# Fewer, larger stores at the end, one load merged, and a tenth pair of tiles turned by VectorE, in a matmul with scale and add

## The chip, the cores and the metric

One core of one Trainium2 chip. The metric is device time in microseconds (us); most executions of one kernel agree within 0.3%. The span is the time from the first to the last of the program's own instructions in the profiled execution; it is about 1.8 us shorter than the device time. All comparisons are between runs of state "fast".

## The reference

```python
batch, m, k, n = 16, 512, 1024, 768
# x [batch, m, k], weight [k, n], add_value [batch, m, n], all float32; scale = 0.1
return (scale * np.matmul(x, weight) + add_value).astype(np.float32)
```

Rows are taken together: 8192 rows, 64 tiles of 128 rows. Read are 61.87 MB, written 25.17 MB.

## The kernel before

The order of all transfers is a list. "x", "w" and "a" load tiles of x, of the weight and of add_value; "o" stores whole tiles, "l" and "r" the left and right columns of one; the numbers are the first tile and how many. All are issued by SyncE, on one queue:

```python
STREAM = [
    ("x", 0, 3), ("w", 0, 2), ("w", 2, 2), ("w", 4, 2), ("x", 3, 1), ("w", 6, 2),
    ("a", 0, 3), ("x", 4, 4), ("a", 3, 1), ("x", 8, 4), ("a", 4, 4), ("x", 12, 4),
    # ... cut ...
    ("o", 40, 8), ("o", 48, 8), ("o", 56, 4), ("o", 60, 1), ("o", 61, 1), ("o", 62, 1),
    ("l", 63, 1), ("r", 63, 1),
]
PAIRS = [14, 19, 24, 29, 34, 39, 44, 49, 54]
```

A tile of x arrives as float32; GpSimd casts it to bfloat16. It then has to be turned for the matmul. For most tiles TensorE transposes it (four 128x128 transposes) and ScalarE copies the result from PSUM. The tiles that PAIRS names (each entry and the one after it) are turned by VectorE in 32x32 blocks, four calls of four instructions per pair, spread over four steps:

```python
def step():
    t = done["step"]
    if t < T - 1:
        for j in range(KJ):                     # KJ = 8
            if j == KJ // 2:
                if t + 1 not in in_pair:
                    transpose(t + 1)            # TensorE, then ScalarE
                cast_to(min(t + AHEAD, done["x"] - 1))     # GpSimd
                if t + 7 in PAIRS:
                    cast_pair(t + 7)            # GpSimd
            product(t, j, BOTH)                 # 128x512 and 128x256
        finish(t, BOTH[0], 0, N)                # VectorE: ao = mm * scale + ao
        for a in range(P // 32):
            if t + 6 - a in PAIRS:
                turn_pair(t + 6 - a, a)         # VectorE
    # ... last tile: columns 0:512 first, then 512:768 ...
```

add_value is loaded into the tile `ao`, overwritten with the result in place and stored from there.

## Time and profile before

| | before |
|---|---|
| device time, median of 3 | 210.95 us |
| span | 209.2 us |
| TensorE / VectorE busy | 196.4 / 131.1 us |
| bytes moved by DMA | 87.2 MB |

In a table by stage the columns are the stretch, its length, busy time (and number of instructions) of each engine, the granted TensorE clock, the DMA share and GB/s. In the list of DMA issues the last number is us from issue to landing.

### The profile page before, as it was taken

What the parts mean: (1) busy time and instruction counts of PE and PEld (TensorE: products, weight loads), DVE (VectorE), ACT (ScalarE), POOL (GpSimd) and SP (SyncE); (2) the same over time, 40 slices, a digit from 0 to 9 for tenths busy, and PEclk for the clock granted to TensorE, in tenths of its full rate; (3) what the DMA queues carried; (4) which work ended last, traced back from release to release, by engine and by line L of the source; (5) the groups of instructions that cost most, each with busy time, mean ns of one, the idle gap of its engine ahead of it and who ended that gap; (6) DMA issues with size and microseconds to landing.
All of it is one profiled execution on the core that took longest, in us unless ns stands there. A gap on an engine that the chain in (4) does not pass through costs nothing.

```text
span 209.2 us, 2988 instructions
## 1 busy us (share of the span) xinstructions
PE 196.4 (94%) x1218; PEld 119.5 (57%) x1218; DVE 131.1 (63%) x223; ACT 49.3 (24%) x52; POOL 63.2 (30%) x69
## 2 busy tenths in 40 slices
PE   7599499999999999999999999999999999999990
PEld 2355256656665666566665666565666656666550
DVE  0545413309969969898697886949994994223340
ACT  2513113233103112113032031121130230332310
POOL 1310536420292090503903606303503039100000
PEclk9889979999999999999999999999999999999997
DMA  6999999999999999999999999999999999999993
GB/s 233 418 431 447 423 408 441 451 445 407 404 481 410 418 432 418 432 451 415 437 417 436 436 421 425 442 434 423 423 432 445 445 409 418 432 447 426 409 402 152
DMA packets 5485, 87.21 MB, mean 417 GB/s; under 512 B 608, under 2 KB 736, under 8 KB 2016
## 3 DMA queue, kind: packets, MB, share of 16 engines
q1 hardware_dynamic: 5472, 87.03, 97.7%
q8 instruction: 9, 0.15, 0.3%
q14 instruction: 4, 0.03, 0.0%
HBM read 61.87 MB, written 25.17 MB: 416 GB/s over the span
## 4 chain that ended last, share of the span: by engine, by line
PE 90%; DMA 3%; DVE 2%; ACT 1%; POOL 0%; issue 0%; ACTq 0%; POOLq 0%
PE mm L168 80%; PE tp L146 10%; DMA xs<-in_x_dram 3%; DVE ao L235 1%; ACT xt L152 1%; DVE ao L204 1%; POOL xb L136 0%; DVE xb L132 0%; DVE ao L176 0%; ACTq L152 0%; POOLq L136 0%
## 5 line engine op out<-in xcount | busy, mean ns | idle before, releaser
L168 PE MATMUL mm<-w_bf,xt 128*128 128x512 bf16 (+1 forms) x736 | 130.8, 331 | 0.6 <-DVE ao L204 0.4
L168 PEld LDWEIGHTS <-xt 128*128 128x128 bf16 x736 | 69.6, 99 | 50.8 <-ACT xt L152 11.4
L176 DVE SCALAR_TENSOR_TENSOR ao<-mm,ao 128x768 f32<-128x768 f32 (+2 forms) x62 | 58.3, 944 | 54.1 <-PE mm L168 35.3
L152 ACT COPY xt<-tp 128x1024 bf16<-128x1024 bf16 (+1 forms) x49 | 46.6, 961 | 146.0 <-PE tp L146 146.0
L120 DVE STREAM_TRANSPOSE vt<-vx 32x256 f32<-32x256 f32 x144 | 62.7, 435 | 6.2 <-POOL vx L109 4.0
L136 POOL CAST xb<-xs 128x1024 bf16<-128x1024 f32 x43 | 43.2, 1040 | 56.2 <-DMA xs<-in_x_dram 46.5
L168 PE MATMUL mm<-w_bf,vt 128*128 128x512 bf16 (+1 forms) x288 | 49.7, 326 | 0.0
L168 PEld LDWEIGHTS <-vt 128*128 128x128 bf16 x288 | 28.2, 98 | 17.5
L109 POOL CAST vx<-xs 128x1024 bf16<-128x1024 f32 x18 | 18.3, 1040 | 53.8 <-DVE vt L120 44.7
L146 PE MATMUL tp<-identity,xb 128*128 128x128 f32 x184 | 28.3, 277 | 5.4 <-POOL xb L136 3.0
L146 PEld LDWEIGHTS tp<-identity,xb 128*128 128x128 f32 x184 | 21.7, 143 | 12.1 <-POOL xb L136 3.4
L104 DVE CAST w_bf<-ao 128x768 bf16<-128x768 f32 x8 | 4.1, 557 | 3.8 <-DMA ao<-in_weight_dram 3.8
L132 DVE CAST xb<-xs 128x512 bf16<-128x512 f32 x3 | 1.9, 696 | 5.6 <-DMA xs<-in_x_dram 5.6
L94 PE MATMUL warm<-zeros 128*128 128x512 bf16 x10 | 4.3, 617 | 1.2 <-DVE zeros L82 1.2
L134 POOL CAST xb<-xs 128x512 bf16<-128x512 f32 x2 | 1.6, 834 | 5.5 <-DMA xs<-in_x_dram 5.5
L94 PEld LDWEIGHTS <-zeros 128*128 128x128 bf16 x10 | 1.3, 140 | 3.4 <-issue 2.2
L204 DVE TENSOR_SCALAR ao<-mm 128x768 f32<-128x768 f32 x2 | 1.8, 952 | 2.3 <-PE mm L168 2.3
L235 DVE TENSOR_TENSOR ao<-ao 128x768 f32<-128x768 f32 x3 | 2.7, 950 | 0.0
L134 ACT CAST xb<-xs 128x512 bf16<-128x512 f32 x1 | 0.6, 618 | 4.8 <-DMA xs<-in_x_dram 4.8
L134 ACT ACT_TABLE_LOAD x1 | 1.3, 1283 | 0.7 <-PEq L279 0.7
L201 ACT ACTIVATE ao<-mm 128x768 f32<-128x768 f32 x1 | 0.8, 817 | 0.0
L82 DVE MEMSET zeros<- 128x256 uint32 x1 | 0.3, 272 | 0.9 <-PEq L279 0.9
(6 smaller groups left out, 0.9 us busy)
## 6 DMA issues: line engine op xcount, KB each, us to landing
xs<-in_x_dram SPq DMA_DIRECT2D x6, 4096.0 KB, 27.3
ao<-in_add_value_dram SPq DMA_DIRECT2D x7, 3072.0 KB, 24.3
out_dram<-ao SPq DMA_DIRECT2D x7, 3072.0 KB, 31.2
xs<-in_x_dram SPq DMA_DIRECT2D x3, 2048.0 KB, 22.0
ao<-in_weight_dram SPq DMA_DIRECT2D x4, 768.0 KB, 9.5
xs<-in_x_dram SPq DMA_DIRECT2D x1, 1536.0 KB, 6.0
ao<-in_add_value_dram SPq DMA_DIRECT2D x1, 1536.0 KB, 23.7
out_dram<-ao SPq DMA_DIRECT2D x1, 1536.0 KB, 11.7
```

Source lines behind the costliest of these rows:

```text
L94: nc.tensor.matmul(warm[:, 0:CUT], zeros[:, 0:P], zeros, start=True, stop=True)
L104: nc.vector.tensor_copy(w_bf[:, j + i, :], ao[:, s + i, :])
L109: nc.gpsimd.tensor_copy(vx[:, i, :], xs[:, (t0 + i) % X_SLOTS, :])
L120: nc.vector.transpose(vt[b:b + 32, :, 32 * a:32 * a + 32], pairs[32 * a:32 * a + 32, :, b:b + 32])
L134: other(xb[:, K // 2:K], src[:, K // 2:K])
L136: nc.gpsimd.tensor_copy(xb, src)
L146: nc.tensor.transpose(tp[:, c, :], pairs[:, c * P:(c + 1) * P], identity)
L152: nc.scalar.copy(dst[:, c:c + q, :, :], src[:, c:c + q, :, :])
L168: nc.tensor.matmul(mm_tiles[t, cols[0]][:, n0:n1], lhs(t, j), w_bf[:, j, n0:n1], start=(j == 0), stop=(j == KJ - 1))
L176: nc.vector.scalar_tensor_tensor(a, mm_tiles[t, part][:, n0:n1], float(scale), a, op0=mybir.AluOpType.mult, op1=mybir.AluOpType.add)
L204: nc.vector.tensor_scalar(ao[:, EARLY_AT + t, :], mm_tiles[t, BOTH[0]][:, 0:N], float(scale), None, op0=mybir.AluOpType.mult)
L235: nc.vector.tensor_add(ao[:, t, :], ao[:, EARLY_AT + t, :], ao[:, t, :])
```

## The change

Its intent: fewer transfers (38 become 34) with longer rows, and less work on TensorE near the end, so that it is done sooner.

```diff
-    ("a", 0, 3), ("x", 4, 4), ("a", 3, 1), ("x", 8, 4), ("a", 4, 4), ("x", 12, 4),
-    ("a", 8, 8), ...
+    ("a", 0, 3), ("x", 4, 4), ("a", 3, 5), ("x", 8, 4), ("x", 12, 4), ("a", 8, 8),
     # ... the middle of the list has the same order ...
-    ("o", 56, 4), ("o", 60, 1), ("o", 61, 1), ("o", 62, 1), ("l", 63, 1), ("r", 63, 1),
+    ("o", 56, 4), ("o", 60, 3), ("o", 63, 1),
-PAIRS = [14, 19, 24, 29, 34, 39, 44, 49, 54]
+PAIRS = [14, 19, 24, 29, 34, 39, 44, 49, 54, 59]
```

(The store of a part of the columns, "l" and "r", goes out of the code.)

## The prediction

> **What bounds the kernel now**
>
> I read the page first (sections 1 to 4), then the table by stage, then SyncE's own waits and its timeline at the end, then the DMA issues of the last 5 us, and last VectorE and GpSimd from 160 us on, where the new pair has to fit.
>
> The page:
>
> ```profile
> span 209.2 us, 2988 instructions
> PE 196.4 (94%) x1218; PEld 119.5 (57%) x1218; DVE 131.1 (63%) x223; ACT 49.3 (24%) x52; POOL 63.2 (30%) x69
> DMA  6999999999999999999999999999999999999993
> q1 hardware_dynamic: 5472, 87.03, 97.7%
> q8 instruction: 9, 0.15, 0.3%
> PE 90%; DMA 3%; DVE 2%; ACT 1%; POOL 0%; issue 0%; ACTq 0%; POOLq 0%
> ```
>
> Two resources look full: TensorE 94%, and the 16 DMA engines 97.7%. The chain of waits gives 90% to TensorE, but that chain ends at the last instruction of a compute engine and does not know what the stores do after it. The table by stage (its last two columns are the DMA share and GB/s) decides:
>
> ```profile
> 60.00:100.00 40.00, 40.00 (x259) 24.72 (x257) 34.23 (x62) 9.11 (x9) 14.68 (x16) 1.00 1.01 432
> 185.00:200.00 15.00, 15.00 (x99) 9.40 (x98) 4.79 (x5) 4.71 (x6) 0.00 (x0) 1.00 1.00 427
> 200.00:205.00 5.00, 3.57 (x22) 1.88 (x20) 2.07 (x3) 0.74 (x1) 0.00 (x0) 1.00 0.95 390
> 205.00:209.20 4.20, 0.00 (x0) 0.00 (x0) 0.00 (x0) 0.00 (x0) 0.00 (x0) 0.70 0.26 97
> ```
>
> DMA is at 1.00 in every stage from 7 us to 200 us. After 205 us no compute engine does anything, and DMA still drains. The end in three views (chain of waits, SyncE's timeline, DMA issues from 203.9 us on):
>
> ```profile
> 203.61 0.42 DVE ao L176
> ```
> ```profile
> 203.45 0.94 SPq L262 DMA_DIRECT2D out_dram<-ao  x2
> ```
> ```profile
> out_dram<-ao SPq DMA_DIRECT2D x1, 128.0 KB, 4.1
> ```
>
> VectorE finishes the last tile at 204.03. The last store (128 KB, issued at 204.06) lands 4.1 us later, at about 208.2, though 128 KB at 432 GB/s is 0.30 us. It waited in the queue behind earlier stores. So the end is set by when the DMA engines have moved 87.03 MB, and TensorE has roughly 3 us of slack there. The span closes about 1 us after the landing, and the measured time is 1.75 us above the span (210.95 against 209.2); I keep both constant.
>
> One more thing from the trace's records: each transfer's landing is 16 completions, one per DMA engine, and they spread. For the last store they run from 205.66 to 208.20, the second last at 207.38. Early on (before 28 us) the spread is 0.33 us. It grows by about 1 to 1.5 us on one engine each time an instruction-refill packet appears: nine of 16,384 bytes on q8, about 20 us apart from 28.0 to 189.9 us, which took 1.0 to 1.1 us each, and smaller ones on q14. After the one at 189.9 the latest engine falls another 1.3 us behind, so it was hit twice. That engine alone sets the last 0.8 us.
>
> **What the Trainium skill says**
>
> - "DMA: Bandwidth & Descriptors", Where 436 GB/s comes from: the SBUF side of the 16 engines tops out at 435 GB/s. The 432 GB/s above agrees; there is nothing left to gain in rate.
> - The same page, Anatomy of one DMA: about 2.0 us fixed plus bytes over 436e9 (it states this for the GpSimd path). Here, from SyncE, the first load (1536 KB) took 6.0 us to land: 3.6 for the bytes and 2.4 fixed. Close. With a queue in front of it the fixed part is hidden, as successive landings show.
> - The same page, Why a DMA increments its semaphore by 16 and not by 1: the engines finish independently. The spread of 2.5 us at the end agrees.
> - "Runtime: NRT & Kernel Launch", Instruction fetch mechanics: refills come in 16 KiB blocks of 256 instructions, "mostly hidden". The nine blocks agree in size and come every 250 to 270 TensorE records; hidden they are not here, since each takes time of a DMA engine that has none spare.
>
> **The change part by part**
>
> 1. *Stores of the tail.* Removed: three of 384 KB, one of 256 and one of 128. Added: one of 1152 KB, one of 384 KB. Same bytes. Each engine handles 8 rows of each transfer. From the packet records (medians): 3072 B 121 ns, 2048 B 84, 1024 B 46, 9216 B 352, and 9 ns for a completion. Per engine before: 8 x (3 x 121 + 84 + 46) = 3944 ns; after: 8 x (352 + 121) = 3784 ns; minus three completions, 27 ns. Saved 0.19 us. Cross-check from landings: the five land over 208.20 - 204.47 = 3.73 us; one 1536 KB store just before took 3.64. So 0.09 is the least, 0.19 the most. It lies on the path.
>
> 2. *add_value 3 to 7 in one.* Before 3072 B + 12288 B rows: 121 + 460 = 581 ns; after one of 15360 B, interpolated between 460 (12288 B) and 912 (24576 B): 573. Eight rows: 0.06 us, plus a completion, 0.07. On the path, since DMA never idles from then on. It moves order: x 8 to 11 now waits behind 1536 KB more of add_value, so it lands at about 34.2 instead of 30.6; add_value 3 lands at about 27.9 instead of 24.2, and 4 to 7 at 27.9 instead of 34.2. Tile 8's TensorE transposes begin at 38.50; GpSimd would cast it by 35.3: 3.2 us to spare. Tile 3's last step on VectorE slips from 26.77 to about 28, and its accumulator is wanted only by tile 6 at about 33. Nothing on the path; tiles 4 and 5 even leave VectorE earlier, as their 6.6 us wait for add_value goes away.
>
> 3. *Tenth pair, tiles 59 and 60.* The order of instructions shows eight transposes (and two ACT copies) fewer on TensorE, sixteen 32x256 transposes more on VectorE, two GpSimd casts into vx in place of two into xb. TensorE: a tile takes 2.63 + 0.44 us with transposes and 7.83 / 3 = 2.61 without (chain), so 2 x 0.46 = 0.9 us earlier at its end. That is not on the path: it moves the issue of the last stores from 201.96 and 204.06 to about 201.1 and 203.15. VectorE: 16 x 435 ns = 7.0 us, in a stretch where it waits on TensorE:
>
> ```profile
> 179.49 0.96 DVE L176 SCALAR_TENSOR_TENSOR ao<-mm,ao 128x768 f32<-128x768 f32 x1 [2.08 <-PE mm L168]
> 170.60 6.95 POOL L136 CAST xb<-xs 128x1024 bf16<-128x1024 f32 x7 [11.69 <-DMA xs<-in_x_dram]
> ```
>
> Its input is late, since x 56 to 63 lands at 170.5. GpSimd casts 56, 57, 58, then 59 and 60, done at 175.6. The first four transposes follow tile 53, whose last step ends at 174.8: VectorE waits 0.8 us, then 1.78 us, so tile 54's step starts at 177.4 instead of 176.45. Tile 55's is late by 0.6, 56's by 0.3, 57's by none; the last transposes end at 185.6. TensorE needs tile 59 at about 188.6, and three accumulators cover the 1 us. Nothing on the path.
>
> Sum: 0.09 to 0.19 plus 0.07, about 0.2 us of 210.95. **Predicted 210.7 us.**
>
> **The rivals**
>
> - *TensorE sets the end.* For it: 94% and the chain. Then 0.9 us from the pair less the loss of the split last store: about 210.0. Against it: 4.1 us to land 128 KB, and 4 us of DMA after the last instruction.
> - *The merged store starves the DMA engines.* The 1152 KB store cannot start before tile 62 is done, at about 201.1, plus some 2.4 us until data moves: 203.5. Engines that are ahead (the first finishes the 1536 KB store at 201.0) idle, which does not matter; the latest finishes it at 204.47 and sees its next work already queued. Margin 1 us, and it exists partly because of the pair. If the fixed part were 1 us longer: 211 to 211.5.
> - *Refills land elsewhere.* The change takes 16 TensorE instructions away and gives VectorE 16. If the refill at 189.9 hit another engine, or dropped out, the end would come at the second-last engine: 0.8 us earlier, 209.9. If one more hit the latest engine: 1.1 to 1.3 us later, about 212. I count on the same nine: about 180 TensorE records follow the last of them, and the 16 removed stand near it. That is the largest uncertainty.
> - *Late VectorE work stalls TensorE.* It would have to cost over 3 us before the DMA end moves. Unlikely.
>
> **Range and chances**
>
> Most mass is within 0.3 us of 210.7; the refill rival stretches downward to 209.9, starving and refills upward to 211.3. Eight in ten: 210.1 to 211.2. A 2% gain is 206.7 us, below what 87 MB at 432 GB/s plus start and end allow (201.5 + 2.4 + 1 + 1.75 = 206.6): under 1%. A 2% loss is 215.2: it needs a stall of over 4 us in the DMA stream, 1%.
>
> **What the profile after would show**
>
> Right: span about 209.0, DMA busy 9 in every slice but the ends, VectorE's last step about 203.1, the last store issued near 203.15 and landing near 208.0 (some 4.8 us); the 1152 KB store issued at about 201.1; TensorE busy about 0.9 to 2 us lower; VectorE about 138; no wait of TensorE longer than now. Wrong: a DMA share visibly under 1.00 before 200 us; a landing of the last store that moves with VectorE's end; another count or place of q8 packets, or an end that moves by 0.8 us or more.

## The result, and the profile after

210.88 us (median of 6, 210.45 to 211.07) against 210.93 (6 runs of the kernel before beside it, 210.59 to 211.10). Ratio 0.9996, 95% interval 0.9984 to 1.0009: the same. A ratio here is the mean time of one kernel's fast runs over that of the other's of the same rounds, so not quite the ratio of the medians.

The page of the changed kernel, the lines that answer to those of before:

```profile
span 209.1 us, 2949 instructions
PE 193.2 (92%) x1187; PEld 117.9 (56%) x1210; DVE 138.2 (66%) x239; ACT 47.2 (23%) x50; POOL 63.3 (30%) x69
DMA  6999999999999999999999999999999999999984
q1 hardware_dynamic: 4896, 87.03, 97.7%
q8 instruction: 9, 0.15, 0.3%
DMA 56%; PE 27%; DVE 8%; POOL 3%; issue 1%; SPq 0%; POOLq 0%; DVEq 0%
```

Of the 3.2 us that TensorE seems to have lost, part is missing records: 31 matmuls fewer are counted, and the change removes 8 (pair_only below, with the same TensorE work and all 1210 matmuls in its trace, is busy 195.2 us). The last line is the chain of waits. It went from 90% TensorE to 56% DMA while the time stayed. One short wait decided that: at 145.12 TensorE had waited 0.75 us for a turned tile, and from there the chain leads through VectorE to a load of add_value that landed at 139.42. tail_51_77 below, whose compute work is the same, has 85% TensorE. The shares of the chain are no proof of what binds.

The table by stage of the changed kernel:

```profile
60.00:100.00 40.00, 39.74 (x253) 24.72 (x257) 34.14 (x62) 9.11 (x9) 14.25 (x16) 1.00 1.01 432
100.00:150.00 50.00, 48.76 (x307) 30.07 (x312) 38.62 (x69) 9.38 (x10) 19.65 (x20) 1.00 1.00 428
185.00:200.00 15.00, 14.89 (x95) 9.26 (x96) 6.00 (x8) 3.63 (x4) 0.00 (x0) 1.00 0.99 424
200.00:205.00 5.00, 2.94 (x18) 1.49 (x16) 2.08 (x3) 0.11 (x1) 0.00 (x0) 1.00 0.90 377
205.00:209.10 4.10, 0.00 (x0) 0.00 (x0) 0.00 (x0) 0.00 (x0) 0.00 (x0) 0.75 0.29 116
```

DMA is as full as before until 200 us (0.99 for 1.00 in 185:200). In 200:205 its share is 0.90 instead of 0.95: the DMA engines that are ahead now wait for the 1152 KB store (the first of them completes the store ahead at 200.98; the first packet of the 1152 KB store starts at 202.16). Over the last 4.1 us the share is 0.29 instead of 0.26. The end, from the chain of waits and from the DMA issues of the last 6 us:

```profile
202.97 0.42 DVE ao L175
```
```profile
out_dram<-ao SPq DMA_DIRECT2D x1, 384.0 KB, 4.7
```

VectorE is done at 203.39, 0.64 us earlier than before; the last store, issued at 203.43, lands 4.7 us later at 208.12, against 208.20. The work ends earlier and the landing does not follow.

The late pair, and add_value 3, from the timelines of VectorE and GpSimd:

```profile
28.12 0.96 DVE L175 SCALAR_TENSOR_TENSOR ao<-mm,ao 128x768 f32<-128x768 f32 x1 [4.56 <-DMA ao<-in_add_value_dram]
...
176.07 1.78 DVE L119 STREAM_TRANSPOSE vt<-vx 32x256 f32<-32x256 f32 x4 [0.96 <-POOL vx L108]
...
194.20 0.96 DVE L175 SCALAR_TENSOR_TENSOR ao<-mm,ao 128x768 f32<-128x768 f32 x1 [2.08 <-PE mm L167]
```
```profile
174.01 2.03 POOL L108 CAST vx<-xs 128x1024 bf16<-128x1024 f32 x2
```

GpSimd has tiles 59 and 60 cast at 176.04; VectorE waits 0.96 us for them, then catches up, and from 191 us on it waits for TensorE again, about 2 us per tile.

### The profile page after: what moved, and what is told of

It reads as the page before. It is cut to its first block, busy times and chain, and to the rows that moved or that the text cites. A ratio compares the mean times of both kernels' runs of the same rounds, so it can differ in the third digit from the quotient of the medians.

```text
span 209.1 us, 2949 instructions
## 1 busy us (share of the span) xinstructions
PE 193.2 (92%) x1187; PEld 117.9 (56%) x1210; DVE 138.2 (66%) x239; ACT 47.2 (23%) x50; POOL 63.3 (30%) x69
## 4 chain that ended last, share of the span: by engine, by line
DMA 56%; PE 27%; DVE 8%; POOL 3%; issue 1%; SPq 0%; POOLq 0%; DVEq 0%
DMA xs<-in_x_dram 28%; PE mm L167 25%; DMA out_dram<-ao 16%; DMA ao<-in_add_value_dram 8%; DVE vt L119 5%; DMA ao<-in_weight_dram 4%; POOL vx L108 3%; PE tp L145 3%; DVE ao L175 2%; POOL xb L135 1%; SPq L101 0%; SPq L247 0%; POOLq L108 0%; POOLq L135 0%; DVEq L175 0%
## 5 line engine op out<-in xcount | busy, mean ns | idle before, releaser
L167 PE MATMUL mm<-w_bf,xt 128*128 128x512 bf16 (+1 forms) x687 | 122.1, 327 | 1.5 <-DVE ao L203 0.4
L167 PEld LDWEIGHTS <-xt 128*128 128x128 bf16 x704 | 66.0, 98 | 48.1 <-ACT xt L151 10.9
L151 ACT COPY xt<-tp 128x1024 bf16<-128x1024 bf16 (+1 forms) x47 | 44.6, 959 | 147.2 <-PE tp L145 147.2
L119 DVE STREAM_TRANSPOSE vt<-vx 32x256 f32<-32x256 f32 x160 | 69.7, 435 | 8.4 <-POOL vx L108 6.0
L135 POOL CAST xb<-xs 128x1024 bf16<-128x1024 f32 x41 | 41.3, 1042 | 55.7 <-DMA xs<-in_x_dram 55.7
L167 PE MATMUL mm<-w_bf,vt 128*128 128x256 bf16 (+1 forms) x314 | 54.6, 325 | 1.7 <-DVE vt L119 1.4
L167 PEld LDWEIGHTS <-vt 128*128 128x128 bf16 x320 | 31.1, 98 | 21.4 <-DVE vt L119 2.1
L108 POOL CAST vx<-xs 128x1024 bf16<-128x1024 f32 x20 | 20.3, 1042 | 53.7 <-DVE vt L119 43.3
L145 PE MATMUL tp<-identity,xb 128*128 128x128 f32 x176 | 27.1, 277 | 5.4 <-POOL xb L135 3.0
L145 PEld LDWEIGHTS tp<-identity,xb 128*128 128x128 f32 x176 | 20.7, 142 | 11.8 <-POOL xb L135 3.4
```

The source lines that it names most:

```text
L108: nc.gpsimd.tensor_copy(vx[:, i, :], xs[:, (t0 + i) % X_SLOTS, :])
L119: nc.vector.transpose(vt[b:b + 32, :, 32 * a:32 * a + 32], pairs[32 * a:32 * a + 32, :, b:b + 32])
L135: nc.gpsimd.tensor_copy(xb, src)
L145: nc.tensor.transpose(tp[:, c, :], pairs[:, c * P:(c + 1) * P], identity)
L151: nc.scalar.copy(dst[:, c:c + q, :, :], src[:, c:c + q, :, :])
L167: nc.tensor.matmul(mm_tiles[t, cols[0]][:, n0:n1], lhs(t, j), w_bf[:, j, n0:n1], start=(j == 0), stop=(j == KJ - 1))
```

## The experiments

Two theories at the start. **DMA:** the time is that of the 16 DMA engines' stream, in particular of the one engine that two instruction refills delayed. **TensorE:** its work sets the end, as the first chain of waits said. All runs with a ratio had 4 to 6 fast runs, and 11 of the kernel before on the same chip.

| run | this, us | before beside it | ratio, 95% |
|---|---|---|---|
| light_pe | 210.90 | 210.94 | 0.9996 (0.9980 to 1.0012) |
| few_refills | 209.77 | 210.94 | 0.9943 (0.9928 to 0.9958) |
| more_refills | 211.00 | 210.94 | 1.0004 (0.9989 to 1.0019) |
| pair_only | 210.93 | 210.94 | 0.9999 (0.9984 to 1.0013) |
| stores_only | 211.02 | 210.89 | 1.0004 (0.9992 to 1.0016) |
| loads_only | 210.77 | 210.89 | 0.9995 (0.9983 to 1.0007) |
| less_dma_before | 208.19 | 210.89 | 0.9870 (0.9857 to 0.9883) |
| less_dma_after | 208.36 | 210.89 | 0.9895 (0.9871 to 0.9920) |
| who_is_late | 210.11 (one run) | 211.19 (one run) | none |
| tail_64_64 | 210.98 | 210.95 | 1.0002 (0.9989 to 1.0014) |
| tail_108_20 | 211.03 | 210.95 | 1.0002 (0.9984 to 1.0021) |
| tail_51_77 | 210.68 | 210.95 | 0.9988 (0.9972 to 1.0005) |

### light_pe: less work on TensorE, the same instructions

A k-step is the product of one tile with 128 of the 1024 values of k: two matmuls, of 512 and of 256 columns.

```diff
 for n0, n1 in cols:
+    if (j == 3 and 3 <= t <= 60) or (j == 5 and 20 <= t <= 35):
+        n1 = n0 + 16
     nc.tensor.matmul(
```

> The changed kernel, with 74 of its 512 k-steps of TensorE cut to 16 columns per matmul (same number of instructions, wrong result on purpose); about 74 x 736 columns[...], over tiles 3 to 60. DMA-bound theory: same bytes, same nine instruction refills, so 210.9 us within 0.3, although VectorE's last step comes earlier or later by whatever the waits for inputs allow. TensorE-bound rival: at least 10 us faster, about 190 to 200 us.

Measured 210.90 us. Its output is wrong, which doesn't matter for the time. Two stages of it, and its last store (the list of issues from 200 us on):

```profile
60.00:100.00 40.00, 37.59 (x276) 22.88 (x274) 35.00 (x63) 9.11 (x9) 14.71 (x16) 1.00 1.01 433
100.00:150.00 50.00, 44.13 (x301) 26.31 (x300) 38.25 (x70) 10.12 (x10) 19.46 (x20) 0.97 1.00 428
```
```profile
out_dram<-ao SPq DMA_DIRECT2D x1, 384.0 KB, 7.8
```

In 100:150 TensorE is busy 44.13 of 50 us where the changed kernel has 48.76 (and the kernel before 49.83), over the whole span 180.3 us for 193.2; VectorE ends at 200.37, and the last store is issued 3 us earlier than in the changed kernel, only to wait 7.8 us instead of 4.7 (landing 208.16). The DMA share stays 1.00. This refutes the TensorE theory.

### few_refills and more_refills: nearly the same arithmetic with fewer and more instructions

```diff
 # few_refills
+    if (j == 3 and 3 <= t <= 60) or (j == 5 and 20 <= t <= 35):
+        return
 # more_refills, for the same (t, j)
+    cols = [(n0 + 16 * i, n0 + 16 * i + 16) for n0, _ in cols_in for i in range(3)]
```

> As light_pe, but the 74 k-steps are left out altogether: 296 TensorE instructions fewer, so by the spacing of about 250 to 270 records the ninth 16 KiB refill should not come (it came with 200 records left). Theory of the latest DMA engine: eight refills, no engine hit twice, the last completion of the last store comes 0.6 to 1.1 us earlier than in light_pe, time about 210.1 us. Rival (refills do not matter, all engines share the load): the same as light_pe within 0.1 us.

> As light_pe, but each of the 74 k-steps is six matmuls of 16 columns instead of two: some 592 TensorE records more, so eleven refills instead of nine. Theory of the latest engine with refills going round eight engines: the tenth and eleventh hit two other engines a second time, so three engines end 3 us or more behind the first instead of one, while the last completion moves by less than 0.5 us: time 210.9 to 211.3. If refills pile on one engine instead: 213 us or more. If refills do not matter: same as light_pe within 0.1.

Both give wrong results on purpose. Section 3 of the two pages:

```profile
q8 instruction: 8, 0.13, 0.3%
```
```profile
q8 instruction: 12, 0.20, 0.4%
```

The ninth refill is gone in the first; the second got twelve, one more than I had counted. How far behind the first DMA engine the sixteen completions of the 1536 KB store (tiles 56 to 59) came, in us, worked out from the completion records of the traces:

```
light_pe, 9 refills      0.00 0.01 0.04 0.10 0.41 0.45 1.28 1.31 1.47 1.48 1.67 1.78 1.79 1.91 1.96 3.27
few_refills, 8 refills   0.00 0.15 0.23 0.23 0.63 0.83 1.55 1.65 1.70 1.74 1.79 1.97 1.97 2.03 2.17 2.28
more_refills, 12 refills 0.00 0.10 0.23 0.28 0.63 0.69 1.62 1.69 1.71 1.73 1.73 2.44 3.00 3.15 3.24 3.38
```

With eight refills no engine is 3 us behind, with nine one is, with twelve four are. That fits refills that go round eight of the engines, where a second hit puts an engine about 1.3 us behind those hit once (3.27 against 1.96). Which engine took a packet the traces don't say, and ten engines, not eight, are over 1.2 us behind in each list; four refills of 8 KB on q14 come on top. The time follows the latest engine: without the ninth refill 209.77 against 210.90, 1.13 us less, beside 0.99 us of difference in the spread. Four late engines instead of one cost nothing more (211.00): the last one ends the kernel, however many come close to it. Among the runs that leave the transfers as they are this is the one effect clear of noise, and it has nothing to do with the change: the change takes 16 TensorE instructions away where some 200 would be needed (an estimate: 173 to 209 TensorE records follow the ninth refill in the profiles of the kernel before, the changed kernel and stores_only).

### pair_only, stores_only, loads_only: one part at a time

```diff
 # pair_only: the kernel before with
-PAIRS = [14, 19, 24, 29, 34, 39, 44, 49, 54]
+PAIRS = [14, 19, 24, 29, 34, 39, 44, 49, 54, 59]
 # stores_only: the kernel before with
-    ("o", 60, 1), ("o", 61, 1), ("o", 62, 1), ("l", 63, 1), ("r", 63, 1),
+    ("o", 60, 3), ("o", 63, 1),
 # loads_only: the kernel before with
-    ("a", 3, 1), ("x", 8, 4), ("a", 4, 4), ("x", 12, 4),
+    ("a", 3, 5), ("x", 8, 4), ("x", 12, 4),
```

> The kernel before with the tenth pair alone (tiles 59 and 60). DMA-bound theory: TensorE and VectorE end about 0.6 to 0.9 us earlier (VectorE at about 203.2 instead of 204.0), the last store lands at the same time within run-to-run noise: 210.9 within 0.3. TensorE-bound rival: 0.6 to 0.9 us faster, 210.0 to 210.3.

> The kernel before with the two merged stores alone, without the tenth pair: the 1152 KB store is issued at about 201.9 and the last one at 204.1. DMA-bound theory: 0.1 to 0.2 us off the stream per engine, but the margin before the latest engine runs dry is only 204.47 - 201.9 - 2.4 = 0.2 us, so anything from 210.7 to 211.2. Rival (merging starves the engines): 211.5 or more, and the last store's landing follows VectorE's end.

> The kernel before with add_value 3 to 7 in one transfer alone. DMA-bound theory: 0.07 us less, unseen in the noise: 210.8 within 0.3. Rival (later x stalls TensorE and through it the stream): over 211.2, and a wait of TensorE for a cast of tile 8 in the profile.

None differs from the kernel before in time. VectorE's end in pair_only and in stores_only (chains of waits):

```profile
202.90 0.42 DVE ao L176
```
```profile
203.95 0.43 DVE ao L175
```

The last stores landed at 208.01 and 208.26. VectorE's end differs by 1.06 us, the landing by 0.25. The share of the DMA engines in stores_only from 202 us on, in slices of 0.175 us:

```profile
DMA  4331109696949593969999499999200000000000
```

The 1152 KB store was issued at 202.30, and its first packet starts at 203.13. Just before that only one or two of the sixteen engines had work left; the latest was busy with the store ahead until 204.18, about 1 us longer. The other fifteen then completed the last store within 0.18 us of each other, and the late one ended the kernel, 1.0 us after the first. So the starving that the prediction had as a rival happens to the engines that do not matter, with a margin of about 1 us for the one that does.

The device times can't show the gains of 0.1 to 0.2 us (stores) and 0.07 us (load) that were expected: the intervals are 0.25 us wide to each side. The completion records can. From the last completion of the 1536 KB store to that of the last store it took 3.72 to 3.74 us in three profiles with five stores in between (before, pair_only, loads_only) and 3.64 to 3.68 in five with two (stores_only, the changed kernel, light_pe, few_refills, more_refills): the merged stores save about 0.08 us. From the first completion of x 4 to 7 to that of x 12 to 15 it took 14.43 to 14.44 us in the four profiles with the split load and 14.36 to 14.40 in the ten with the merged one: about 0.06 us.

### less_dma_before and less_dma_after: what lies behind the DMA bound

The load of add_value 40 to 47 is left out of either kernel:

```diff
-    ("a", 40, 8),
```

> The kernel before without the load of add_value 40 to 47 (3 MB, 7.28 us of the DMA stream; wrong result on purpose). If DMA alone set the time, 7.3 us faster: 203.7. My theory says TensorE is right behind: its end stays at 204.0 for VectorE, then the last store (128 KB) needs about 2.4 us plus 0.3 with an empty queue: lands at 206.7 or so, 1.5 us earlier than now, time 209.2 to 209.6.

> The changed kernel without the same load. TensorE-bound here as well: VectorE ends 0.6 us earlier than before (203.4) but the last store is 384 KB instead of 128 (0.9 instead of 0.3 us): lands at about 206.7, time 209.2 to 209.6, so no better than less_dma_before within 0.3. Rival: where TensorE bounds, the pair's 0.6 to 0.9 us shows in full: 208.5.

Measured 208.19 and 208.36 us: not 7.3 us faster but 2.7 and 2.5, so another limit lies close behind, as expected; I had put it 1 us too high. The end of less_dma_before, then of less_dma_after (stage from 185 us on, and the last stores):

```profile
185.00:200.00 15.00, 15.00 (x100) 9.50 (x100) 4.79 (x5) 4.85 (x5) 0.00 (x0) 1.00 0.76 318
```
```profile
out_dram<-ao SPq DMA_DIRECT2D x2, 384.0 KB, 2.3
out_dram<-ao SPq DMA_DIRECT2D x1, 256.0 KB, 2.0
out_dram<-ao SPq DMA_DIRECT2D x1, 128.0 KB, 1.8
```
```profile
185.00:200.00 15.00, 15.00 (x98) 9.16 (x96) 5.18 (x6) 3.50 (x4) 0.00 (x0) 1.00 0.63 268
```
```profile
out_dram<-ao SPq DMA_DIRECT2D x1, 1152.0 KB, 4.2
out_dram<-ao SPq DMA_DIRECT2D x1, 384.0 KB, 3.0
```

Here TensorE is busy throughout 185:200 and DMA is not (0.76 and 0.63): TensorE sets the end. A store now waits for nothing, and 384 KB land in 2.3 us, of which 0.9 is for the bytes; so the fixed part of a store is 1.4 us, not the 2.4 that I had taken from the first load. That is the 1 us by which I was off. In this regime the change shows no gain either (208.36 for 208.19). The profiled executions suggest a reason: VectorE ends at 203.16 instead of 203.49, but the last store lands 3.0 us after that instead of 1.9, as it is three times as large and stands behind 1152 KB that could not start before tile 62. So the merged stores would give back what the pair gains. That is argued: no run has the pair alone here, and the profiled execution of less_dma_after took 208.92 us, 0.56 above its median.

### who_is_late: which DMA engine is the last one

The Trainium skill ("DMA: Bandwidth & Descriptors", Why a DMA increments its semaphore by 16 and not by 1) says that a transfer from SyncE runs on the largest number of engines up to 16 that divides its slowest dimension, and on the lowest-numbered ones. That allows a probe: tile 60 in pieces of different numbers of partitions.

```diff
-    ("o", 60, 3), ("o", 63, 1),
+    ("o", 60, 1), ("o", 61, 2), ("o", 63, 1),
+    cuts = [0, 2, 6, 14, 26, 40, 128] if s == 60 else [0, 128]
+    for p0, p1 in zip(cuts, cuts[1:]):
+        nc.sync.dma_start(rows(out_v, s, n)[p0:p1], ao[p0:p1, k:k + n, :])
```

> The changed kernel (right result), with tile 60 stored in six pieces of 2, 4, 8, 12, 14 and 88 partitions and tiles 61 and 62 in one. Not a speed test: a piece of p partitions should run on few DMA engines (2, 4, 8, 12, 14 and 11 of them), so its number of completions, and which of the sixteen delays they carry, tells whether the DMA engine hit by two refills is a low-numbered one. If it is above the first 8, a later kernel can give it less of the last stores and end up to 0.8 us sooner; if it is among the first 8, it can't be spared in this way. Time 210.9 to 211.5.

From the completion records, after the 1536 KB store, whose last two engines completed at 203.39 and 204.35:

```
partitions   2      4      8      12     14     88
completions  2      4      8      12     14     11
last one at  201.93 203.08 203.59 203.79 204.51 204.68
```

The counts agree with the skill. The piece on 12 engines was complete at 203.79, before the latest engine had finished the store ahead (204.35), so that engine is not among the first 12; the piece on 14 shows it. By chance the probe itself gave that engine one row of tile 60 instead of eight, and the single run took 210.11 us against 211.19. That made a faster kernel look possible; one run is no proof of it.

### tail_64_64, tail_108_20, tail_51_77: less work for the late engine

Tile 60 in two pieces, cut at partition 64, 108 or 51; the rest as in who_is_late. All three results are right.

> Control: the changed kernel (right result) with tile 60 stored alone, in two pieces of 64 partitions, and tiles 61 and 62 in one store. Each piece runs on all sixteen DMA engines, 4 rows each, so no load is shifted; three more transfers. Latest-engine theory: as the changed kernel, 210.9 within 0.3. Rival (it was the smaller or earlier first piece, not the shift of load, that made the six-piece kernel faster): about 210.1 like it.

> Tile 60 in pieces of 108 and 20 partitions: 12 and 10 DMA engines, so the engines 12 to 15 get no row of it and 0 to 9 get 11 instead of 8 (right result). From the completions of the six-piece run the latest engine is number 12 or 13, 1.0 us behind the next. Worked out: it ends at 204.35 + 24 x 0.114 = 207.1, the latest of the others at 203.39 + 35 x 0.114 = 207.4, against 208.1 of the changed kernel: time 210.2, 0.3 to 0.4% faster. Rival (identity wrong or changing from run to run): 210.9, or 211.2 if the latest is among the first ten.

> Tile 60 in pieces of 51 and 77 partitions: engines 0 to 2 with 17 rows each, and 0 to 10 with 7 each; 11 to 15 get none. Engines 0 to 2 were 2.6 us ahead by the six-piece run (201.1, 201.8, 201.7), so they take most of it. Worked out: engines 0 to 2 end at 201.8 + 48 x 0.114 = 207.2, 3 to 10 at 203.39 + 31 x 0.114 = 206.9, the latest at 207.1: about 0.9 us before the changed kernel: time 210.0, 0.4% faster. Rival: 211 or more if engines 0 to 2 are not early in most runs.

The control does what it should (210.98, all five runs within 210.90 to 211.15). The other two miss: 211.03 and 210.68, neither clear of the kernel before. In the profiled executions the last stores do land earlier: at 207.55 with the cut at 108 (time 210.42) and at 207.67 with the cut at 51 (210.57). But the six times of that kernel are 210.42, 210.91, 210.60, 211.65, 211.15 and 211.31, a spread of 1.23 us where the control has 0.25. That fits a late engine that changes from one execution to the next: about 210.2 was expected where it is number 12 to 15, 211.2 where it is one of the first ten, and times near both occur. It is argued, not shown: only one execution of each kernel has its completions recorded, and these do not show the engine move. In tail_108_20 the piece on the first 12 engines was complete at 204.48, before the latest engine had finished the store ahead (204.82), so that engine is none of the first 12, as in who_is_late. By this reading the single fast run of who_is_late was luck of the draw; why the six times spread stays open, and no version that beats both kernels was found. A version with some 200 fewer TensorE instructions might, by few_refills, gain 0.5%; I know of no way to get there with a right result, and it was not tried.

## Why the prediction was right

- **The bound.** DMA with about 3 us of slack on TensorE: light_pe (TensorE busy 12.9 us less, no time saved) and the two less_dma kernels (7.28 us of transfer less, 2.5 to 2.7 us saved) show it from both sides.
- **Part 1, stores,** 0.09 to 0.19 us: 0.08 by the completion records, so the cross-check with one large store came close and the sum of packet times was more than twice too much. The time doesn't resolve it. Measured for the whole change is 0.04% less with an interval of 0.16% less to 0.09% more, that is 0.34 us less to 0.19 us more; the 0.2 us of the sum lies inside, and so does nothing at all. The range of 210.1 to 211.2 held an unchanged time too: the hit confirms the bound, not the 0.2.
- **Part 2, load:** landings came as worked out (34.04 for x 8 to 11, 28.02 for add_value 3 to 7, VectorE's step of tile 3 at 28.12), no compute step was held up in a way that reached the end, and the stream gained 0.06 us for 0.07.
- **Part 3, pair:** VectorE 138.2 us busy for 138, GpSimd's casts done at 176.04 for 175.6, tile 54's step at 177.88 for 177.4. VectorE's end moved from 204.03 to 203.39, 0.64 us for the 0.9 expected. Over four profiles without the pair that end lies at 203.5 to 204.4, over seven with it (light_pe, few_refills and more_refills left out) at 202.8 to 203.4: means 203.9 and 203.2.
- **The mis-sized terms:** the fixed part of a store was taken as 2.4 us from the first load; on an idle queue it is 1.4, and of that only 0.83 passes before data moves (202.16 less 201.33). So the starving rival had a margin of 1.9 us (the latest engine's last packet ahead ended at 204.05), not 1. And "no wait of TensorE longer than now" was wrong: it waited 0.62 and 0.75 us for turned tiles near 57 and 145 us. These belong to older pairs. Near 57, TensorE came earlier to the same tile: in 24:60 the granted clock was 1.00 there and 0.95 in the profile before, and loads_only, without the new pair and also at 1.00, waits 0.81 us at the same place. Near 145, the chain leads to the load of add_value that landed at 139.42 (138.75 before), its latest engine 2.62 us behind the first (1.93 before). Neither cost time, as TensorE has slack.
- **The refill rival** was the right worry: nine refills in both kernels, and one engine 3.5 us behind the first in both, so the time stayed. The ninth came at 187.2 us and not 189.9, which the prediction had named as a sign of being wrong; it comes at 187.3 in stores_only and at 189.1 in loads_only, and the end did not move with it.
- **A slip:** the 2% gain of 206.7 us is not below the 206.6 that the prediction sets against it. No chance or range hangs on the 0.1 us.

## What to carry to other kernels

When the last store takes several times its own bytes' time to land, the DMA queue ends the kernel, and a faster end of the compute engines buys nothing; look for the landing before believing a chain of waits that says 90% TensorE. Merging stores saved about 0.08 us in all where the queue was full. Where it was empty the last landing came 1.2 us later after the last compute step (3.04 for 1.87 us, one profile each); a merged store starts only when its last tile is done. Sixteen DMA engines end when the latest does, so look at the spread of the completions, and don't build on which engine it was in one profile.

## What the Trainium skill lacked or had wrong

- "Runtime: NRT & Kernel Launch", Instruction fetch mechanics: it calls the cost of crossing a 16 KiB block "mostly hidden". In this DMA-bound kernel the ninth block of TensorE costs 1.13 us (209.77 without it, 210.90 with it, nearly the same arithmetic).
- No page has it: on which DMA engines refills fall. 8, 9 and 12 refills left 0, 1 and 4 engines 3.0 us or more behind the first at the 1536 KB store, as if they went round eight engines, and the latest engine ends the kernel.
- "DMA: Bandwidth & Descriptors", Queues, rings and completion order: refills are put in queue row 14. Here the 16,384-byte packets, which come every 238 to 270 TensorE records (kernel before), ran on q8; only the 8 KB ones ran on q14 (9 and 4 packets in the span).
- The same page, Anatomy of one DMA: about 2.0 us fixed, for the GpSimd path alone. From SyncE on an idle queue a 384 KB store shows 1.4 us (2.3 less 0.9 for the bytes), the first load of the kernel 2.4.
